# The forward half of the decays' rows made by ScalarE as scaled copies of the mask, in a gated DeltaNet encoder layer

## The chip, the cores and the metric

The kernel runs on one core of a Trainium2 chip. The metric is the device time of one execution in microseconds (us). A core has four compute engines that run side by side, each with its own queue of instructions taken in order: TensorE (PE in the profile: matmuls and transposes; its weight loads, PEld, are shown apart), VectorE (DVE), ScalarE (ACT) and GpSimd (POOL). A fifth, SyncE (SP), only issues DMA transfers here. Engines wait for each other through semaphores.

## The reference, cut to what matters

One layer of a bidirectional encoder is applied to a prompt of 1024 tokens and to a sample of 256, with the same weights. A combined projection feeds two groups of heads: four gated DeltaNet heads, in which a chunked delta rule runs once forward and once backward with separate decays, and four heads of grouped-query attention. An output projection and an MLP follow.

```python
def _gated_delta_chunked(q, k, v, g, beta):          # g <= 0: log of the decay; one direction
    gc = jnp.cumsum(to_chunks(g), axis=-1)
    diff = gc[..., :, None] - gc[..., None, :]
    decay = jnp.where(lower_incl, jnp.exp(jnp.where(lower_incl, diff, 0.0)), 0.0)
    kk = jnp.einsum('bhnid,bhnjd->bhnij', k_beta, kc) * decay
    tri = jnp.eye(CHUNK) + jnp.where(strict, kk, 0.0)
    sol = triangular_solve(tri, [v_beta, k_beta * exp(gc)], lower, unit_diagonal)
    qk = jnp.einsum('bhnid,bhnjd->bhnij', qc, kc) * decay
    ...                                               # scan over chunks with a 128x128 state

def _gated_deltanet(...):
    qkv = silu(depthwise_conv(qkv, conv_w))           # five taps
    q, k = _l2norm(q) * GDN_DK ** -0.5, _l2norm(k)
    o = o_f + flip(o_b)                               # one scan per direction, own g and beta each
    return rmsnorm(o) * gdn_norm_w * silu(z)

def _layer(x, ...):
    p = rmsnorm(x) @ w_in                             # 1024 -> 3088 columns
    mix = concat(_gated_deltanet(...), _axial_gqa(...)) @ w_out
    x = x + rmsnorm(mix)
    return x + rmsnorm(square(relu(rmsnorm(x) @ w_up)) @ w_down)
```

What the change touches is `decay`: for each head, direction and chunk, the exponential of the difference of two running sums of `g`, and zero on the other side of the diagonal.

## The kernel before, in words

**Tiles and stages.** The 1280 tokens lie as ten tiles of 128 (eight of the prompt, two of the sample), and a tile is also the chunk of the delta rule. Values that go through TensorE at full width are split into a rounded high part and the rest (`split`: the high part by ScalarE, L79, the low part by VectorE, L80), and a product takes three matmuls. The kernel runs in stages: the input norm and the gates (until about 85 us), then the projections with everything that prepares the DeltaNet heads (until about 520 us), then attention with the scans, then the output projection and the MLP. The change lies in the second stage.

**The second stage.** It is built from generators that each do one part of the work for one head: K (`gdn_qk`, L453: project, convolve and normalise key and query), V (`gdn_v`, L497: the same for the value), E (`gdn_e`, L511: decays and the matrices A and C made from them), S (`gdn_sub`, L542) and L (`gdn_lev`, L569: the triangular inverse, by VectorE in blocks of 32 first, then by TensorE), and a (`att_proj`, L383: a projection for attention). A table of steps, `ORDER` (L39 to L43), says in which order their pieces are written; `K1 E0 K1 S0`, for instance, writes a piece of head 1's key and query, one of head 0's decays, and so on. A scheduler then orders the instructions of each engine by what they need and by that order, so an edit in one generator can move rows of others in every queue.

**A projection** (`proj_T`, L358 and following): 24 matmuls for each of three stretches of tokens (pt, L370 to L372), copied out by ScalarE (cp, L373). The convolution starts on ScalarE (L443, L444), goes through three steps on VectorE (L446), a sum on GpSimd (L447), a tanh on ScalarE (L448) and a last step on VectorE (L449). TensorE then transposes the result (kt L462, qt L476, vt L505).

**The decays** (`gdn_e`). A head has five groups of two tiles, so there are 20 groups in all. For each group one PSUM tile, pe, of 128 x 512 holds forward (d = 0) and backward (d = 1) for two tiles; two such tiles alternate. Into each half go three matmuls: one writes the mask of large negative values (nmask, L519), two add the differences of the running sums (L525). The latter multiply a constant triangle (strict) with R, which the profile calls ER: the mask of kept positions (`incl`, 128 x 128) times g of the row. `gr` holds g as a high and a low part, so one R has four blocks of 128 x 128: high and low (i) for two tiles (j). Summed along the partitions by the matmul, column c of R becomes the sum of g over the rows between. There is one buffer of R (`bufs=1`), used in turn by the forward and the backward half: the forward half is made by GpSimd, the backward half by VectorE, each in one instruction of 128 x 512 (L521). ScalarE takes the exponential of pe (E, L526). Then for each of the two tiles TensorE makes the products of keys with keys and queries (pk, L531), and VectorE makes A (L532) and C (L534) from pk and E. C goes into the inverse, A to memory in `vis_d`, where the scans fetch it later (vis, L655).

**The start of the third stage.** SP loads the normalised keys, the first queries and the values (ax, L666) and the first chunks of the scans (vis, L655); the former are split (k_hi, q_hi, v_hi) ahead of the first scores (ps_s, L715) and the scans' products (p, L813 and following).

Of the kernel before, what the change touches and what calls it, by code (L numbers as in the profile page):

```python
# [13 lines left out]
AF = mybir.ActivationFunctionType  # L14
ALU = mybir.AluOpType
# [46 lines left out]
def build(ctx, tc, I, O):  # L62
    nc = tc.nc
    V, S, G, T, SP = nc.vector, nc.scalar, nc.gpsimd, nc.tensor, nc.sync
# [9 lines left out]
    def f32(ap):  # L74
        return ap.bitcast(F32)
# [38 lines left out]
    scale = 128.0 ** -0.5  # L114
# [123 lines left out]
    incl = gc.tile([128, 2, 128], F32, name="incl")  # L238
# [92 lines left out]
    gr = gc.tile([128, 2, NT, 8], F32R, name="gr")  # L331
# [5 lines left out]
    for d in range(2):  # L337
        gd = gg[:, :, 4 * d:4 * d + 4]
# [15 lines left out]
    def col(t):  # L354
        return slice(t * 128 + (2 if t >= NPR else 0), t * 128 + (2 if t >= NPR else 0) + 128)
# [155 lines left out]
    def gdn_e(h):  # L511
        qk, sc = qks[h], sca[:, h]

        C = gp.tile([128, NT, 2, 128], F32, tag="C", name="C", bufs=2)
        for t0, n in ((0, 2), (2, 2), (4, 2), (6, 2), (8, 2)):
            E = gp.tile([128, 2, 2, 128], F32, tag="E", name="E", bufs=2)
            pe = tr_tile("pe").rearrange("p (d j c) -> p d j c", d=2, j=2)
            for d in range(2):
                T.matmul(pe[:, d], lhsT=identr, rhs=nmask[:, 1 - d:2 - d].to_broadcast([128, 2, 128]), start=True, stop=False)  # L519
                R = gp.tile([128, 2, 2, 128], F32R, tag="ER", name="ER", bufs=1)  # L520
                (G if d == 0 else V).tensor_tensor(  # L521
                    R, incl[:, d][:, None, None, :].to_broadcast([128, 2, 2, 128]),
                    f32(gr[:, :, t0:t0 + 2, 4 * d + h])[:, :, :, None].to_broadcast([128, 2, 2, 128]), ALU.mult)
                for i in range(2):
                    T.matmul(pe[:, d], lhsT=(r_gt, r_lt)[d], rhs=R[:, i], start=False, stop=(i == 1))  # L525
            S.activation(E, pe, AF.Exp)  # L526
            A = gp.tile([128, 2, 2, 128], F32, tag="A", name="A", bufs=1)
            for j in range(n):
                t = t0 + j
                pk = tr_tile("pk")  # L530
                T.matmul(pk[:, 0:256], lhsT=qk[:, 1, col(t)], rhs=qk[:, :, col(t)], start=True, stop=True)  # L531
                V.tensor_tensor(A[:, j], E[:, :, j], pk[:, None, 0:128].to_broadcast([128, 2, 128]), ALU.mult)  # L532
                for d in range(2):
                    V.scalar_tensor_tensor(C[:, t, d], pk[:, 128:256], sc[:, t, d:d + 1], E[:, d, j], ALU.mult, ALU.mult)  # L534

            SP.dma_start(out=vis_d[h][:, t0:t0 + n, 0], in_=A[:, :, 1])
            SP.dma_start(out=vis_d[h][:, t0:t0 + n, 7], in_=A[:, :, 0])
            if t0 < 8:
                yield
        Cs[h] = C  # L540
# [28 lines left out]
    def gdn_lev(h):  # L569
# [63 lines left out]
        SP.dma_start(out=vis_d[h][:, :, 8], in_=C[:, :, 0])  # L633

    FN = dict(K=gdn_qk, V=gdn_v, E=gdn_e, S=gdn_sub, L=gdn_lev, a=att_proj)
    parts = {}
    for step_ in ORDER.split():
# [752 lines left out]
    for s in range(NS):  # L1390
        n, i = divmod(s, 7)
# [135 lines left out]
```

## Time and profile before

| what | value |
|---|---|
| median of three runs | 1722.2 us (1721.96 to 1723.77) |
| the profiled execution | 1718.87 us |
| its span, first to last instruction | 1717.1 us, mean granted TensorE clock 0.987 |
| TensorE busy (PE) | 1615.6 us, 94% of the span |
| weight loads (PEld) | 1380.5 us, 80% |
| VectorE busy (DVE) | 1276.5 us, 74% |
| ScalarE busy (ACT) | 851.2 us, 50% |
| GpSimd busy (POOL) | 703.1 us, 41% |
| DMA | 252.68 MB, 147 GB/s on average |

The profile is one execution, recorded by the hardware. Shares over the whole span are an average over stages with different limits, so the second stage has to be read by itself. In the rows that follow, `cy<-cp,cw` means that tile cy is written from tiles cp and cw; `x20 | 28.4, 1422` is a count, the busy time of all of them in us and the mean of one in ns; what stands behind it is the idle time of that engine just before them, and the work whose end closed most of it. A row of the timeline has the start in us, the duration in us, the engine and the instruction; in square brackets stands how long the engine had been idle ahead of it and what ended that.

### The profile page before, as it was taken

The numbers are of one execution on the slowest core, as the hardware profiler recorded it, in microseconds if no ns is written. First come the engines' busy times: TensorE is split into PE (matmuls) and PEld (weight loads), VectorE is DVE, ScalarE is ACT, GpSimd is POOL, SyncE is SP. The second block draws the span as 40 slices with busy tenths as digits, with TensorE's granted clock in tenths as the row PEclk, the third lists the DMA queues.
The fourth block names the chain that finished last, engine by engine and source line by source line (L and its number), as shares of the span: only waits on it lengthen the run. The fifth ranks groups of instructions, "written<-read, shape, count | busy, mean of one in ns | idle before, by whom it ended". The sixth has DMA issues, their size and how long they took to land. (4 is left out here: it accounts for less than half of the span.)

```text
span 1717.1 us, 27988 instructions
## 1 busy us (share of the span) xinstructions
PE 1615.6 (94%) x9799; PEld 1380.5 (80%) x9799; DVE 1276.5 (74%) x2570; ACT 851.2 (50%) x1937; POOL 703.1 (41%) x637
## 2 busy tenths in 40 slices
PE   7999899898997999889998999999999999999996
PEld 5777777777776888668877999999998888888885
DVE  7546798996755878885759659555797888887876
ACT  5236567554345767674446446544564333333412
POOL 1212231321114334440103634644335778878852
PEclk9999999999998999999999999999999999999998
DMA  7113335455457766245333545444666444444244
GB/s 221 67 44 108 106 100 143 123 143 154 129 149 241 269 206 193 81 163 168 106 121 116 167 136 177 150 134 138 199 212 209 147 139 148 141 128 147 78 138 150
DMA packets 208779, 252.68 MB, mean 147 GB/s; under 512 B 35073, under 2 KB 163391, under 8 KB 208639
## 3 DMA queue, kind: packets, MB, share of 16 engines
q1 hardware_dynamic: 208495, 250.77, 46.4%
q8 instruction: 77, 1.26, 0.3%
q14 instruction: 63, 0.52, 0.1%
q0 software_dynamic: 144, 0.13, 0.0%
HBM read 159.75 MB, written 91.10 MB: 146 GB/s over the span
## 5 line engine op out<-in xcount | busy, mean ns | idle before, releaser
L1165 PE MATMUL pd<-mh,uhl 128*128 128x320 f32 x892 | 278.0, 312 | 9.8 <-DVE uhl L1156 9.6
L1164 PE MATMUL pd<-mh,uhl 128*128 128x320 f32 x892 | 275.4, 310 | 1.6 <-ACT uhl L1155 1.6
L1166 PE MATMUL pd<-ml,uhl 128*128 128x320 f32 x892 | 276.1, 310 | 0.0
L1313 DVE TENSOR_TENSOR acc<-acc,pd 128x512 f32<-128x512 f32 x330 | 207.3, 679 | 48.6 <-PE pd L1309 48.2
L1307 PE MATMUL pd<-dhi,fhi 128*128 128x512 f32 x490 | 192.2, 392 | 0.7 <-DVE acc L1315 0.7
L1308 PE MATMUL pd<-dl,fhi 128*128 128x512 f32 x490 | 192.3, 392 | 0.0
L1309 PE MATMUL pd<-dhi,flo 128*128 128x512 f32 x490 | 191.9, 392 | 0.0
L1165 PEld LDWEIGHTS pd<-mh,uhl 128*128 128x128 f32 x892 | 168.3, 189 | 12.7 <-DVE uhl L1156 12.7
L371 PE MATMUL pt<-h_lo,whi 128*128 128x512 f32 (+1 forms) x480 | 177.4, 370 | 0.0
L370 PE MATMUL pt<-h_hi,whi 128*128 128x512 f32 (+1 forms) x480 | 177.3, 369 | 0.0
L372 PE MATMUL pt<-h_hi,wlo 128*128 128x512 f32 (+1 forms) x480 | 177.2, 369 | 0.0
L1164 PEld LDWEIGHTS pd<-mh,uhl 128*128 128x128 f32 x892 | 167.8, 188 | 2.7 <-ACT uhl L1155 2.7
L1166 PEld LDWEIGHTS pd<-ml,uhl 128*128 128x128 f32 x892 | 168.3, 189 | 0.0
L1289 ACT CAST fhi<-fr 128x1280 fp32r<-128x1280 f32 x49 | 62.1, 1267 | 200.9 <-PE pd L1308 114.5
L1210 POOL TENSOR_TENSOR s<-u,u 128x320 f32<-128x320 f32 x31 | 29.2, 941 | 254.9 <-ACT u L1174 249.3
L1279 POOL TENSOR_TENSOR dl<-dw,dhi 128x1024 fp32r<-128x1024 f32 x47 | 118.5, 2522 | 28.2 <-ACT dhi L1278 28.2
L1156 DVE TENSOR_TENSOR uhl<-us,uhl 128x512 fp32r<-128x512 f32 x88 | 86.3, 983 | 37.1 <-ACT uhl L1155 36.3
L730 POOL TENSOR_TENSOR P<-P,sm 128x512 f32<-128x512 f32 (+1 forms) x72 | 73.5, 1040 | 95.0 <-DVE sm L728 47.7
L1307 PEld LDWEIGHTS pd<-dhi,fhi 128*128 128x128 f32 x490 | 92.0, 188 | 22.0 <-issue 1.1
L1309 PEld LDWEIGHTS pd<-dhi,flo 128*128 128x128 f32 x490 | 92.0, 188 | 20.7
L1308 PEld LDWEIGHTS pd<-dl,fhi 128*128 128x128 f32 x490 | 92.0, 188 | 20.4
L1173 ACT ACTIVATE u<-u 128x320 f32<-128x320 f32 x128 | 60.2, 470 | 93.0 <-DVE u L1200 39.2
(368 smaller groups left out, 4098.0 us busy)
## 6 DMA issues: line engine op xcount, KB each, us to landing
fr<-r_d SPq DMA_DIRECT2D x49, 640.0 KB, 3.9
vis<-vis_d SPq DMA_DIRECT2D x64, 384.0 KB, 4.1
uraw<-in_w_up SPq DMA_DIRECT2D x22, 1024.0 KB, 5.3
r_d<-s SPq DMA_DIRECT2D x128, 160.0 KB, 1.8
r_d<-u SPq DMA_DIRECT2D x96, 160.0 KB, 1.8
dw<-in_w_down SPq DMA_DIRECT2D x28, 512.0 KB, 4.3
wraw<-in_w_in SPq DMA_DIRECT2D x48, 256.0 KB, 3.9
x<-in_x_prompt SPq DMA_DIRECT2D x16, 512.0 KB, 3.5
```

Of the source, the lines that this page charges most:

```text
L370: T.matmul(pm[:, :n], lhsT=whi, rhs=h_hi[:, k, t0:t0 + n], start=(k == 0), stop=False)
L371: T.matmul(pm[:, :n], lhsT=whi, rhs=h_lo[:, k, t0:t0 + n], start=False, stop=False)
L372: T.matmul(pm[:, :n], lhsT=wlo, rhs=h_hi[:, k, t0:t0 + n], start=False, stop=(k == KD - 1))
L1156: V.tensor_tensor(lo, ua[n][UP[i][0]], f32(hi), ALU.subtract)
L1164: T.matmul(pm, lhsT=w[0][:, k], rhs=mh[b, i][:, k], start=(k == 0), stop=False)
L1165: T.matmul(pm, lhsT=w[1][:, k], rhs=mh[b, i][:, k], start=False, stop=False)
L1166: T.matmul(pm, lhsT=w[0][:, k], rhs=ml[b, i][:, k], start=False, stop=(k == 3))
L1279: last["pool"] = leng.tensor_tensor(lo, raw, f32(hi), ALU.subtract)
L1307: T.matmul(pm, lhsT=r[0][:, k, tk], rhs=w[0][:, k], start=(k == 0), stop=False)
L1308: T.matmul(pm, lhsT=r[0][:, k, tk], rhs=w[1][:, k], start=False, stop=False)
L1309: T.matmul(pm, lhsT=r[1][:, k, tk], rhs=w[0][:, k], start=False, stop=(k == Q - 1))
L1313: last["dve"] = V.tensor_tensor(half(t, d), half(t, d), pm, ALU.add)
```

## The change

For the forward half (d = 0) of each group, the one GpSimd instruction that made R is replaced by four ScalarE instructions, one for each block of 128 x 128: an activation with function Copy that reads the mask `incl` and multiplies each partition's row by a scale of its own, a column of `gr`. The backward half stays one VectorE instruction, and the tile, its single buffer and the matmuls that read it stay as they are.

```diff
@@ -518,9 +518,14 @@
             for d in range(2):
                 T.matmul(pe[:, d], lhsT=identr, rhs=nmask[:, 1 - d:2 - d].to_broadcast([128, 2, 128]), start=True, stop=False)
                 R = gp.tile([128, 2, 2, 128], F32R, tag="ER", name="ER", bufs=1)
-                (G if d == 0 else V).tensor_tensor(
-                    R, incl[:, d][:, None, None, :].to_broadcast([128, 2, 2, 128]),
-                    f32(gr[:, :, t0:t0 + 2, 4 * d + h])[:, :, :, None].to_broadcast([128, 2, 2, 128]), ALU.mult)
+                gd = f32(gr[:, :, t0:t0 + 2, 4 * d + h])
+                if d == 0:
+                    for i in range(2):
+                        for j in range(2):
+                            S.activation(R[:, i, j], incl[:, d], AF.Copy, scale=gd[:, i, j:j + 1])
+                else:
+                    V.tensor_tensor(R, incl[:, d][:, None, None, :].to_broadcast([128, 2, 2, 128]),
+                                    gd[:, :, :, None].to_broadcast([128, 2, 2, 128]), ALU.mult)
                 for i in range(2):
                     T.matmul(pe[:, d], lhsT=(r_gt, r_lt)[d], rhs=R[:, i], start=False, stop=(i == 1))
             S.activation(E, pe, AF.Exp)
```

The instructions of TensorE, VectorE and SP are the same in number (8824, 2573 and 826 in the program); ScalarE goes from 1628 to 1708, GpSimd from 643 to 623. Lines behind the edit are five higher: the matmul of R is L525 before and L530 now, the exponential L526 and L531, pk L531 and L536, C L534 and L539. The scheduler's order differs from the first group of head 0 up to about two thirds of attention and is the same from there on. Three places follow; a number behind x counts rows in a row that are alike.

ScalarE's queue where the second head's groups (E1) begin, before:

```order
L373 COPY cp<-pt 128x256
L526 ACTIVATE E<-pe 128x512
L443 ACTIVATE cy<-cp,cw 128x1282
L444 ACTIVATE qk<-cp,cw 128x1282
L526 ACTIVATE E<-pe 128x512
L373 COPY cp<-pt 128x512
L526 ACTIVATE E<-pe 128x512
L373 COPY cp<-pt 128x512
L79 CAST whi<-wraw 128x512 x2
L373 COPY cp<-pt 128x256
L444 ACTIVATE qk<-cp,cw 128x1282
L548 ACTIVATE Cc<-C 32x640 x4
```

The same place now, with the copies of the mask as rows of L525:

```order
L373 COPY cp<-pt 128x256
L443 ACTIVATE cy<-cp,cw 128x1282
L444 ACTIVATE qk<-cp,cw 128x1282
L79 CAST whi<-wraw 128x512 x2
L531 ACTIVATE E<-pe 128x512
L525 ACTIVATE ER<-incl,gr 128x128 x4
L531 ACTIVATE E<-pe 128x512
L525 ACTIVATE ER<-incl,gr 128x128 x4
L531 ACTIVATE E<-pe 128x512
L525 ACTIVATE ER<-incl,gr 128x128 x4
L448 ACTIVATE qk<-cy 128x1282
L553 ACTIVATE Cc<-C 32x640 x4
```

The start of the convolution has moved ahead of the groups, and three groups stand together, each E ahead of the next group's four copies; behind the last of them comes the tanh.

TensorE's queue at the end of the second head's groups, before (pe and pk belong to the groups, pt to a projection; fifteen more rows of pt follow before the next pe):

```order
L371 MATMUL pt<-h_lo,whi 128x256
L372 MATMUL pt<-h_hi,wlo 128x256
L519 MATMUL pe<-nmask,identr 128x256
L525 MATMUL pe<-ER,strict 128x256 x2
L519 MATMUL pe<-nmask,identr 128x256
L370 MATMUL pt<-h_hi,whi 128x512
L371 MATMUL pt<-h_lo,whi 128x512
L372 MATMUL pt<-h_hi,wlo 128x512
```

The same place now:

```order
L530 MATMUL pe<-ER,strict 128x256 x2
L536 MATMUL pk<-qk 128x256
L519 MATMUL pe<-nmask,identr 128x256
L530 MATMUL pe<-ER,strict 128x256 x2
L519 MATMUL pe<-nmask,identr 128x256
L536 MATMUL pk<-qk 128x256
L530 MATMUL pe<-ER,strict 128x256 x2
L536 MATMUL pk<-qk 128x256
L519 MATMUL pe<-nmask,identr 128x256
L530 MATMUL pe<-ER,strict 128x256 x2
L519 MATMUL pe<-nmask,identr 128x256
L462 MATMUL kt<-ident,qk 128x128 x4
```

Two groups now follow each other with no matmul of a projection between; those matmuls stand elsewhere in the queue.

SP's queue at the change from the second to the third stage, before (L410 stores attention's values, L433 a rotated key, L666 loads a key, query or value, L655 a scan's chunk; the keys take three loads, the fourth is the first queries):

```order
L666 DMA ax<-arot_d 128x512
L410 DMA arot_d<-avn 128x512
L666 DMA ax<-arot_d 128x512
L410 DMA arot_d<-avn 128x512
L410 DMA arot_d<-avn 128x256
L666 DMA ax<-arot_d 128x256
L666 DMA ax<-arot_d 128x512
L433 DMA arot_d<-araw 128x1280
L655 DMA vis<-vis_d 128x512
```

The same place now:

```order
L410 DMA arot_d<-avn 128x512 x2
L410 DMA arot_d<-avn 128x256
L671 DMA ax<-arot_d 128x512 x2
L671 DMA ax<-arot_d 128x256
L660 DMA vis<-vis_d 128x512
L433 DMA arot_d<-araw 128x1280
L660 DMA vis<-vis_d 128x384
L660 DMA vis<-vis_d 128x128
L660 DMA vis<-vis_d 128x512
L660 DMA vis<-vis_d 128x384
L660 DMA vis<-vis_d 128x128
L671 DMA ax<-arot_d 128x512 x3
```

The keys' loads stand together behind the last value stores, and the first queries (the first row of the last x3) come behind six loads of scan chunks.

## The prediction

> **What bounds the kernel now.** I began with busy time in three stretches: the gates and the first head, the middle of the projections, their tail. Columns are busy microseconds, instructions in brackets.
>
> ```profile
> core 0: us, PE busy (x) PEld busy (x) DVE busy (x) ACT busy (x) POOL busy (x), PEclk, DMA share, GB/s
> 85.00:200.00 115.00, 105.51 (x551) 84.40 (x550) 68.18 (x133) 61.96 (x178) 23.02 (x26) 0.99 0.32 89
> 200.00:400.00 200.00, 179.56 (x1418) 144.56 (x1417) 181.65 (x417) 117.74 (x318) 54.63 (x135) 0.97 0.46 126
> ```
>
> From 200 to 400 us TensorE (90% busy) and VectorE (91%) are both nearly full, ScalarE is at 59%, GpSimd at 27%. So here the longest chain changes hands between two engines, and only what makes one of them wait counts. Next the waits of TensorE, and of VectorE for ScalarE, from 85 to 440 us: total, times, longest.
>
> ```profile
> PE pe L519 <- DVE C L534: 7.5, 5, 2.5
> PE vt L505 <- DVE vT L449: 5.7, 3, 2.1
> PE pe L525 <- DVE ER L521: 1.2, 1, 1.2
> ...
> DVE wlo L80 <- ACT whi L79: 11.9, 12, 2.5
> DVE qk L449 <- ACT qk L448: 11.3, 4, 4.5
> ```
>
> TensorE waits for VectorE. For ER it waited once, and that ER was VectorE's: it never waited for GpSimd's rows. VectorE in turn waits for ScalarE's results. Last the groups that the edit touches: count, busy us and mean ns, idle time before them.
>
> ```profile
> L521 POOL TENSOR_TENSOR ER<-incl,gr 128x512 fp32r<-128x512 f32 x20 | 28.4, 1422 | 71.2 <-PE pe L525 69.8 <-DVE wlo L80 1.4
> L467 ACT ACTIVATE kn<-kt,cum 128x128 f32<-128x128 f32 x80 | 22.5, 397 | 0.3 <-DMA vis_d<-kn 0.3
> L443 ACT ACTIVATE cy<-cp,cw 128x1282 f32<-128x1282 f32 x12 | 16.6, 1380 | 2.4 <-DVE qk L449 2.4
> ```
>
> GpSimd's 69.8 us idle before ER is the one ER buffer not yet read, and costs nobody anything unless something needed is queued behind.
>
> **Part by part.** *Added on ScalarE.* Twenty groups get four copies of 128x128 with a scale per row: 80 instructions. The kn row is the same count of the same form, reading PSUM: 22.5 us, 1.12 a group. From below, L443's time per element (16.6/12/1282 = 1.08 ns) gives 80 x 128 x 1.08 = 11 us; from above, 80 full durations of 397 ns give 32 us. I take 22.5, the nearest row. The copies add no wait of their own: the ER buffer comes free with the same matmuls (L525, backward half) that E (L526) waits for, and E stands ahead of the next copies in ScalarE's queue. What they delay is behind them. In the order, 9 of the 20 groups have, as the next row that is not an E, a weight split, a copy of a projection, a tanh or the inverse's first copy, all on somebody's path: 9 x 1.12 = 10.1 us. The other eleven are followed by squares, kn and the like, which the 41% idle time of the stretch hides; without that cover they would cost another 12.3. That idle time absorbs as much of the 10.1, and 59% passes on, since VectorE already waits for ScalarE: **+6.0** (0 to 10.1).
>
> *Removed from GpSimd.* No engine waited for the result, but VectorE was slowed while it was made. Start, us, instruction:
>
> ```profile
> 239.50 1.67 POOL L521 TENSOR_TENSOR ER<-incl,gr 128x512 fp32r<-128x512 f32 x1
> ...
> 127.46 1.68 DVE L446 SCALAR_TENSOR_TENSOR cy<-cp,cw,cy 128x1282 f32<-128x1282 f32 x1 [0.58 <-ACT cy L443]
> ...
> 236.68 0.40 DVE L564 TENSOR_TENSOR Rm<-Rm,prod 80x247 f32<-80x247 f32 x1
> 238.24 1.43 DVE L563 TENSOR_TENSOR prod<-Rm 80x240 f32<-80x240 f32 x1
> 240.19 1.25 DVE L564 TENSOR_TENSOR Rm<-Rm,prod 80x240 f32<-80x240 f32 x1
> ...
> 397.69 1.02 DVE L89 TENSOR_SCALAR nah<-nax 128x10 f32<-128x10 f32 x1
> ```
>
> The two products at 238.24 and 240.19, which take 0.40 otherwise, took 1.43 and 1.25. Twelve VectorE instructions were so lengthened under an ER, from the one at 127.46 to the one at 397.69; each less the median of its shape, they sum to 8.7 us. VectorE is the one waited for about half the time (it and TensorE are equally full), so **-4.3** (-8.7 to 0). The Trainium skill ("SBUF — State Buffer", Who interferes with whom) says that a GpSimd instruction reading SBUF and a VectorE one with two SBUF inputs exclude each other for a whole instruction. By that rule up to all 28.4 us of ER could have stood in VectorE's way, an estimate, half of it -14.2; the trace agrees on who blocks whom and gives 8.7 as the size.
>
> GpSimd's queue also gets shorter. Once a conv sum stood behind an ER:
>
> ```profile
> 176.98 1.60 POOL L521 TENSOR_TENSOR ER<-incl,gr 128x512 fp32r<-128x512 f32 x1 [4.45 <-PE pe L525]
> 178.54 3.40 POOL L447 TENSOR_TENSOR cy<-cy,qk 128x1282 f32<-128x1282 f32 x1
> ```
>
> ScalarE's tanh and then TensorE's transposes wait for that sum. Half of 1.6, as above: **-0.8** (-1.6 to 0).
>
> *Moved: the second head's groups.* Two groups now stand in TensorE's queue with no projection matmul between, at a place where VectorE interleaves the groups with the triangular inverse. VectorE's pace per group there is the distance of its ERs; TensorE's own work per group is the three lower rows over 20.
>
> ```profile
> 212.54 0.68 DVE L521 TENSOR_TENSOR ER<-incl,gr 128x512 fp32r<-128x512 f32 x1
> 226.39 0.68 DVE L521 TENSOR_TENSOR ER<-incl,gr 128x512 fp32r<-128x512 f32 x1
> ...
> L531 PE MATMUL pk<-qk 128*128 128x256 f32 x80 | 26.5, 419 | 3.2 <-DVE prod L563 2.3 <-ACT E L526 0.7
> L525 PE MATMUL pe<-ER,strict 128*128 128x256 f32 x80 | 18.2, 307 | 1.2 <-DVE ER L521 1.2
> L519 PE MATMUL pe<-nmask,identr 128*128 128x256 f32 x40 | 13.0, 326 | 7.8 <-DVE C L534 7.5
> ```
>
> Pace 13.85/2 = 6.9, work 57.7/20 = 2.9: 4.05 us of idle in each group, 8.1 for two. The projection matmuls that stood there run later instead, where TensorE had these gaps:
>
> ```profile
> 242.90 0.66 PE L462 MATMUL kt<-ident,qk 128*128 128x128 f32 x4 [1.87 <-DVE qk L449]
> 258.16 1.10 PE L531 MATMUL pk<-qk 128*128 128x256 f32 x4 [2.30 <-DVE prod L563]
> 274.53 0.66 PE L505 MATMUL vt<-ident,vT 128*128 128x128 f32 x4 [2.03 <-DVE vT L449]
> ```
>
> They fill up to 6.2 us: **+1.9** (-6.2, if VectorE keeps ahead, to +8.1). A gap also slows what follows it:
>
> ```profile
> 201.39 0.39 PE L371 MATMUL pt<-h_lo,whi 128*128 128x512 f32 x1
> 204.30 0.38 PE L519 MATMUL pe<-nmask,identr 128*128 128x256 f32 x1 [2.52 <-DVE C L534]
> 206.71 0.63 PE L371 MATMUL pt<-h_lo,whi 128*128 128x512 f32 x1
> ```
>
> After 2.52 us of idle the same matmul takes 0.63 for 0.39. New gaps and filled ones both carry this, so I let it cancel. The Trainium skill ("TensorE: Matmul & The Clock Gate", HAM oscillation) puts the limit at gaps over about 3.4 us. By that only the new gaps would pay; the row at 204.30 shows a shorter gap paying, and decides.
>
> *Moved: the change to attention.* SP's queue now has the first query load behind the last value stores and six vis loads.
>
> ```profile
> 526.08 0.80 PE L715 MATMUL ps_s<-k_hi,q_hi 128*128 128x512 f32 x1 [6.22 <-ACT q_hi L79]
> 530.59 1.06 PE L813 MATMUL p<-vis 128*128 128x128 f32 x4
> ...
> 524.20 2.78 SPq L655 DMA_DIRECT2D vis<-vis_d  x6
> ```
>
> TensorE waits 6.22 us for that query today; six issues take 2.78, so the wait grows by as much, less four L813 matmuls put ahead in the meantime (1.06 us): **+1.7** (0 to +2.8).
>
> The sum is 6.0 - 4.3 - 0.8 + 1.9 + 1.7 = +4.5. The profiled execution took 1718.87 (span 1717.1 and 1.77 around it): 1723.4. The median of the runs lies 3.3 higher, at 1722.2: **1726.7**. Nothing after the attention's first two thirds is reordered, and TensorE is full there, so I let the difference stand to the end.
>
> **Rivals.** *A, the relief wins (faster).* ScalarE's idle time takes the copies, at most 1.0 of the 10.1 passes, and VectorE gains the whole 8.7: -8.7 - 0.8 + 1.0 + 1.9 + 1.7 = -4.9, so 1717.3. For it: VectorE is the fullest engine from 200 to 400. Against: the 23 us that VectorE waits for ScalarE between 85 and 440 us. It decides once under 2.4 of the 10.1 passes and the relief is whole. This is also what the port rule of the Trainium skill's "SBUF — State Buffer" leads to. *B, nothing measurable.* Groups wait for whichever of the two full engines is behind, the terms cancel: 1722.2, 0.2% (3.4 us) either way, about what a measurement of this kernel can tell from no change. For it: no wait for GpSimd's ER exists, and TensorE can lose little to an engine 59% busy. *C, ScalarE's queue becomes the wait.* All 10.1 pass, nothing of the 8.1 comes back: 10.1 - 4.3 - 0.8 + 8.1 + 1.7 = +14.8, so 1737. For it: three groups of copies stand in a row ahead of a tanh. Against: ScalarE's 82 idle us in the stretch. That the edit does not do what it says would mean copies much dearer than kn; that is C as well, at up to 32 us.
>
> **How the numbers follow.** My forecast (slower by 3.4 to 9 us) has 0.36, A 0.28, B 0.27, C 0.09. So faster 0.28, same 0.27, slower 0.45. The range takes A with no loss at the two moved places (-4.9 - 3.6 = -8.5, 1713.7, less a little) up to C: 1712 to 1737. The forecast's own range is 1725.6 to 1731.
>
> **What would show it.** Right: about 80 ER copies of 22 us in all on ScalarE; ScalarE above 63% between 200 and 400; VectorE's lengthened products gone; gaps of 3 to 5 us on TensorE inside the second head's groups; a first ps_s wait above 6.2. Wrong: VectorE's wait for whi and tanh unchanged with fewer TensorE gaps than now (A), or all gaps merely moved (B).

## The result: slower by 1.8%

The changed kernel takes 1753.2 us (median of 3 runs, 1752.9 to 1754.7) against 1722.2: a ratio of 1.0177, 95% interval 1.0159 to 1.0195, or 31 us. That lies outside the predicted range (1712 to 1737), on the side that had 0.45. A ratio compares a kernel with runs of the kernel before made beside it, so it need not be that of the medians given.

The profiled execution has a span of 1751.1 us. The stretches of the prediction, and the two behind them, in the changed kernel (columns as there):

```profile
85.00:200.00 115.00, 107.06 (x562) 86.72 (x560) 71.34 (x139) 70.85 (x208) 15.57 (x23) 0.99 0.31 84
200.00:400.00 200.00, 168.78 (x1407) 134.04 (x1410) 167.76 (x396) 125.81 (x342) 30.75 (x117) 0.89 0.44 118
400.00:520.00 120.00, 109.12 (x957) 86.59 (x958) 72.68 (x195) 43.88 (x141) 15.24 (x36) 0.94 0.42 122
520.00:560.00 40.00, 28.16 (x160) 22.60 (x158) 13.10 (x27) 14.43 (x45) 6.96 (x3) 0.82 0.61 195
```

From 200 to 400 us TensorE falls from 90% to 84% busy and VectorE from 91% to 84%: both wait more, so neither became the bound. ScalarE, which got the work, reaches 62.9%, where above 63% was forecast. The granted clock in that stretch is 0.89 for 0.97. The waits of the same window, 85 to 440 us, and the new group:

```profile
DVE wlo L80 <- ACT whi L79: 29.4, 9, 7.7
DVE qk L449 <- ACT qk L448: 13.9, 5, 4.5
PE pe L519 <- DVE C L539: 7.1, 4, 3.2
PE qt L476 <- ACT gj L379: 6.1, 1, 6.1
PE pk L536 <- DVE qk L449: 3.4, 1, 3.4
```

```profile
L525 ACT ACTIVATE ER<-incl,gr 128x128 fp32r<-128x128 f32 x80 | 26.7, 406 | 0.0
```

The copies cost 26.7 us of ScalarE where 22.5 were forecast. TensorE waits for R twice, 0.4 us in all, whichever engine makes it. VectorE's waits for weight splits and tanh have grown (29.4 for 11.9 and 13.9 for 11.3 us), and TensorE has two new single waits, of 6.1 and 3.4 us.

TensorE runs the same 9799 rows in both traces. Its busy time goes from 1615.6 to 1629.7 us and the rest of the span from 101.5 to 121.4, so of the 34 us by which the profiled execution is longer, 20 are idle time and 14 are the same matmuls taking longer, at a mean granted clock of 0.973 for 0.987.

To see where the time goes I took TensorE's matmuls in both traces, counted each with the spacing its kind has in a run without gaps, and noted when the same amount of work had been done (a reckoning of work). Changed kernel less before, in us:

| time before | work done | changed less before | what lies between |
|---|---|---|---|
| 177 | 150 | -1.6 | |
| 216 | 180 | -4.9 | the changed kernel is ahead |
| 236 | 200 | +8.9 | end of the second head's groups |
| 323 | 270 | +9.4 | |
| 334 | 280 | +21.1 | fourth head's query, third head's value |
| 460 | 380 | +12.9 | 8 us won back |
| 471 | 390 | +20.3 | attention's projections, prk |
| 515 | 430 | +23.1 | |
| 591 | 490 | +33.6 | change to attention |
| 726 | 610 | +33.5 | nothing more |

So there are four places. Two are those of the prediction, at 14 and 10 us instead of 1.9 and 1.7; two it didn't have. The sizes of these two, 11.7 and 7.4 us here, hang on the spacing that is taken for each kind: with the median of all spacings in the trace they come out at 16.0 and 10.6, and more is won back between them. What the first three share is seen in the busy time of the projections alone (tile pt) in three stretches, before and then changed:

```profile
core 0: us, PE busy (x), PEclk, DMA share, GB/s
...
220.00:235.00 15.00, 13.41 (x62) 1.00 0.14 40
...
325.00:345.00 20.00, 14.05 (x66) 0.91 0.43 111
...
460.00:485.00 25.00, 23.03 (x110) 1.00 0.46 139
```

```profile
core 0: us, PE busy (x), PEclk, DMA share, GB/s
...
220.00:235.00 15.00, 0.42 (x1) 0.66 0.15 44
...
325.00:345.00 20.00, 2.37 (x21) 0.64 0.37 103
...
460.00:485.00 25.00, 12.30 (x60) 0.80 0.30 104
```

Before, projections that wait for nobody fill TensorE's queue beside the groups and the convolutions. Now they stand elsewhere, and where VectorE's, GpSimd's and ScalarE's chains are long, TensorE has nothing else in its queue. Counting the projection matmuls that ran ahead of the same row in both traces says where they went. From the second head's third group to the third head's first mask 81 ran before and 34 run now; of the 47 that are missing, 17 had been done ahead (ahead of that third group 440 have run for 423, which fits the lead of 4.9 us) and 30 come later. At the second place, from the first of the fourth head's query transposes to the first of the third head's value transposes, 69 ran before and 7 run now, and all of the missing come later. At the third, behind attention's last prk rows, 28 ran before and none now, and all had been done ahead. At the first place the gaps are these rows of the changed kernel; before, TensorE is idle for 0.1 us over the same work:

```profile
230.08 0.58 PE L519 MATMUL pe<-nmask,identr 128*128 128x256 f32 x1 [3.17 <-DVE C L539]
...
233.65 1.11 PE L462 MATMUL kt<-ident,qk 128*128 128x128 f32 x4 [2.35 <-DVE qk L449]
```

### The profile page after: what moved, and what is told of

The parts are those of the page before. It is cut to its first block, busy times and chain, and to the rows that moved or that the text cites. A ratio compares the mean times of both kernels' runs of the same rounds, so it can differ in the third digit from the quotient of the medians.

```text
span 1751.1 us, 28001 instructions
## 1 busy us (share of the span) xinstructions
PE 1629.7 (93%) x9799; PEld 1390.0 (79%) x9799; DVE 1275.6 (73%) x2570; ACT 873.8 (50%) x2017; POOL 671.3 (38%) x617
## 5 line engine op out<-in xcount | busy, mean ns | idle before, releaser
L1170 PE MATMUL pd<-mh,uhl 128*128 128x320 f32 x892 | 278.2, 312 | 10.3 <-DVE uhl L1161 10.1
```

The lines of the kernel that those rows point to most:

```text
L1170: T.matmul(pm, lhsT=w[1][:, k], rhs=mh[b, i][:, k], start=False, stop=False)
```

## Experiments

**How an order is held.** The order of all five queues was recorded from each of the two programs, and an edge that only sets the order of issue (no semaphore, no wait) was put from each instruction to its predecessor in the record. The forward half's instructions have no edge and stand where the scheduler puts them. Apart from these, the rows of every engine in run 1's trace stand in the order of the kernel before, and those of run 2 in the order of the changed kernel. At the end of the program (excerpt):

```diff
+    for line in zlib.decompress(base64.b85decode(HELD)).decode().splitlines():
+        e, *runs = line.split()
+        q = [i for i in nc.cur_bb.bb.instructions if str(i.engine) == "EngineType." + e ... and i.name not in FREE]
...
+                    tc.add_manual_dep(q[k], prev.name, mybir.DependencyInfo(
+                        mybir.DependencyClass.NoSync, mybir.DependencyReason.DATA), reason="held order")
```

Theory O: the time is lost by the new order of the queues, whichever engine makes the rows. Rival E: it is lost by ScalarE's copies.

**1. The edit in the old order.**

> The edit as it is (four ScalarE copies for the forward half), but every engine's queue held to the order it had before; only the copies are free to stand where the scheduler puts them. Theory O (the loss of 31 us is the new order of the queues): 1715 to 1727 us, within 0.3% of before, with no TensorE wait over 3 us between 215 and 240 or between 320 and 350 us. Rival E (the loss is ScalarE's added 25 us of copies, wherever they stand): 1745 us or more.

Measured: 1721.3 us, 1.0002 of before (0.9991 to 1.0012). TensorE's longest wait is 0.7 us between 215 and 240 and 2.1 between 320 and 350, and the projections are where they were (tile pt, this kernel):

```profile
220.00:235.00 15.00, 13.53 (x53) 1.00 0.26 71
325.00:345.00 20.00, 14.92 (x72) 1.00 0.56 155
460.00:485.00 25.00, 22.57 (x108) 1.00 0.45 133
```

**2. The old engine in the new order.** The edit is undone (excerpt):

```diff
-                            S.activation(R[:, i, j], incl[:, d], AF.Copy, scale=gd[:, i, j:j + 1])
+                (G if d == 0 else V).tensor_tensor(R, ...)
```

> The other corner: GpSimd makes the forward half as before, and every engine's queue is held to the order that the changed kernel has; only GpSimd's 20 instructions are free. Theory O: 1745 to 1760 us, with the changed kernel's long TensorE waits near 225, 335, 472 and 545 us. Rival E: 1718 to 1727 us.

Measured: 1754.7 us, 1.0203 (1.0179 to 1.0228). Together the two settle it: with the old order held, moving the work to ScalarE costs nothing that can be measured; with the engine held, the order costs 35 us with GpSimd's rows and some 30 with ScalarE's copies (1.0177 against 1.0002). The intervals of these last two overlap. Rival E falls. No run held the old order and changed nothing else, but run 10 is near to it, at 0.9998.

**3. and 4. Price and relief, each alone, in the old order.** ScalarE does the copies as well, into a tile D that nobody reads (3); the forward half is made once, and all groups read that tile, so that 19 groups lack their own decays (4):

```diff
+                    D = gp.tile([128, 2, 2, 128], F32R, tag="ED", name="ED", bufs=1)
+                            S.activation(D[:, i, j], incl[:, d], AF.Copy, scale=gd[:, i, j:j + 1])
```

```diff
+                if d == 0:
+                    R = R0
```

> The price of the copies alone: GpSimd and VectorE make R as before, and ScalarE makes the four copies a second time into a tile that nobody reads, at the places that they have in the run of the edit in the old order; all queues are held to the old order. Theory O: 0 to 6 us over before, 1722 to 1728. Rival E: 20 us or more over before.

> The relief alone: the forward half is made once, by GpSimd, and all 20 groups read that one tile (the decays of the forward direction are left out of the computation but for one group's); queues held to the old order. Theory O: 0.8 to 9 us under before, 1713 to 1721, by VectorE's products that GpSimd no longer lengthens. If the relief is worth nothing: 1720 to 1724. Rival E says nothing of this one.

Measured: the copies alone 1724.8 us, 1.0023 (1.0012 to 1.0035), +3.9 us; without the forward half 1714.1 us, 0.9952 (0.9935 to 0.9969), -8.3 us. Both are as expected. They don't add up to run 1: 3.9 - 8.3 = -4.4 against +0.3. Run 4 also frees the one R buffer of its forward use, so that VectorE's ER no longer waits at all (9.1 us before); whether that is the 4.7 us between them was not separated.

**5. to 7. Old order up to a cut, then the new one**, with ScalarE's copies: a queue is the old record's part ahead of the cut, followed by what is left of the new record.

> ScalarE's copies; all queues in the old order up to the 190th group of three projection matmuls (about 250 us, behind the second head's groups), then what is left in the new order. Theory P (the loss sits at separate places, each with its own wait: near 225, 335, 472 and 545 us): the first place is gone, which leaves what the trace lost after it, 33 - 7 = 26 us: about 1747 us. Rival W (one early loss, and the later waits only follow from it): 1727 us or less.

> The same with the cut at the 310th group of projection matmuls, about 360 us, behind the third head's groups and the fourth head's query. Theory P: 33 - 20 = 13 us are left, about 1734 us. Rival W: 1724 us or less.

> The same with the cut at the 460th group of projection matmuls, about 505 us: only the change to attention is in the new order. Theory P: 33 - 23 = 10 us over before, about 1731 us. The prediction's own term for this place was 1.7 (0 to 2.8): 1721 to 1724. Rival W: 1722.

Measured: 1757.6 (ratio 1.0225), 1760.7 (1.0236) and 1728.3 us (1.0056, 1.0035 to 1.0077). The first two miss both theories. The same reckoning of work shows why: the cut itself costs, 9 us behind 250 us and about 25 us behind 360 us, where TensorE waits 6.8 and 7.05 us in one piece. That the new order takes work for done that the old one had left for later would explain it, and was not tested. Behind the join the places come back, each with its size: from work 270 to 280 the first of the two loses 12.1 us (changed kernel 11.7), from work 380 to 390 they lose 7.5 and 7.4 (changed kernel 7.4). So the places don't hang on what went before them, which is against rival W; theory P's totals missed because a join has a price of its own. The third is as theory P has it: the change to attention costs 9.6 us by the ratio. By the reckoning it is 1.9 us behind before at work 430 and 9.5 at 610, so its join costs next to nothing.

**8. New up to 212 us, then old.**

> The other way round: the new order up to its 150th group of projection matmuls, about 212 us, where the changed kernel was 4.9 us ahead of before, then the old order. Theory P: the lead is kept, about 1716 us. Rival L (the lead is work done early that the old order then waits for): 1720 to 1724 us.

Measured: 1714.1 us, 0.9965 (0.9952 to 0.9979): 6 us faster than before by the ratio, some 36 faster than the changed kernel by the two ratios. The projections are back in their places (tile pt, this kernel):

```profile
220.00:235.00 15.00, 14.04 (x68) 1.00 0.18 52
...
325.00:345.00 20.00, 13.70 (x66) 0.91 0.42 103
...
460.00:485.00 25.00, 21.56 (x100) 1.00 0.50 142
```

**9. The same with GpSimd's rows**, the edit undone as in run 2.

> The faster mixture of orders (new up to about 212 us, then old) with GpSimd making the forward half as in the kernel before. If the 5 us won there are the order's alone: 1713 to 1716 us, as with ScalarE's copies. If they are the engine's (rival A of the prediction, VectorE no longer lengthened by GpSimd): 1719 us or more.

Measured: 1719.6 us, 0.9988 (0.9976 to 0.9999). That is the time named for the engine (1719 or more), though the order is still worth some 2 us without it; by the ratios of runs 8 and 9, whose intervals just overlap, the engine is 4 of the 6 us. The spans of the two profiled executions, 1711.2 and 1712.6, say 1.4, but this kernel's profiled execution (1714.35 us) is the second shortest of twelve. So ScalarE's copies may be a small gain in this order, up to some 4 us and not clear of noise, and they are nothing in the old one.

**10. The clock behind a long wait**, on the kernel before in its own order:

```diff
+            for _ in range(34 if not pend[0] and not halves else 0):
+                T.matmul(pm[:, 0:128], lhsT=ident, rhs=ident, start=True, stop=True)
```

> The price of the lowered clock behind one long wait, on the kernel before: 34 transposing matmuls of the identity (128x128), whose result the first scores overwrite, stand in TensorE's queue in the 6.2 us in which it waits for the first queries; all else in the old order. If the lowered clock costs time there (granted 0.50 to 0.76 between 525 and 535 us): the clock stays at 1.00 and 2 to 4 us are won, 1715 to 1717. If VectorE and ScalarE set the pace there anyway: 0, 1719 us, with the clock up all the same.

Measured: 1720.1 us, 0.9998 (0.9986 to 1.0010). The windows of before, then of this kernel:

```profile
525.00:530.00 5.00, 3.79 (x8) 2.59 (x9) 1.42 (x3) 0.62 (x1) 1.28 (x1) 0.50 0.97 326
530.00:535.00 5.00, 4.55 (x21) 3.73 (x21) 3.43 (x9) 3.60 (x10) 1.22 (x2) 0.76 0.79 268
```

```profile
525.00:530.00 5.00, 5.00 (x42) 4.75 (x41) 0.76 (x2) 1.02 (x2) 1.27 (x1) 1.00 0.95 287
530.00:535.00 5.00, 4.55 (x23) 3.11 (x21) 3.70 (x9) 3.39 (x9) 0.76 (x1) 1.00 1.02 356
```

The clock stays at 1.00 and nothing is won beyond the 2 us that the interval leaves open. The added matmuls ran 7.8 us, about 1 us past the queries' arrival, so at most that much was hidden. Behind them, from 535 to 540 us, VectorE is busy for 4.83 of 5 us before and for all 5 here, which fits the second expectation. At this place the lowered clock is a sign of the wait and not its price; at the others it wasn't tried, and the 14 us by which the changed kernel's matmuls take longer are the most that it can have cost TensorE there.

**11. One instruction moved in the new order.** The timeline of the changed kernel at the place of the fourth head's query and the third head's value, which is the third of the four vT (the expectation below calls it the fourth head's) (excerpt):

```profile
327.46 0.28 PE L519 MATMUL pe<-nmask,identr 128*128 128x256 f32 x1
...
331.14 1.19 PE L536 MATMUL pk<-qk 128*128 128x256 f32 x2 [3.41 <-DVE qk L449]
...
337.06 0.28 ACT L379 ACTIVATE gj<-qt 128x128 bf16<-128x128 f32 x1
...
337.86 2.88 POOL L447 TENSOR_TENSOR cy<-cy,vT 128x1282 f32<-128x1282 f32 x1 [2.89 <-DVE prod L568]
...
338.07 2.75 DVE L569 TENSOR_TENSOR Rm<-Rm,prod 80x60 f32<-80x60 f32 x1
...
340.77 1.27 ACT L448 ACTIVATE vT<-cy 128x1282 f32<-128x1282 f32 x1 [3.34 <-POOL Rm L570]
341.87 0.22 DVE L569 TENSOR_TENSOR Rm<-Rm,prod 80x60 f32<-80x60 f32 x1
341.95 0.26 ACT L379 ACTIVATE gj<-qt 128x128 bf16<-128x128 f32 x1
342.35 1.12 PE L476 MATMUL qt<-ident,qk 128*128 128x128 f32 x4 [6.12 <-ACT gj L379]
```

TensorE's next four transposes need the buffer that the fourth square (gj, 341.95) reads. That square stands behind the value's tanh, which waits for GpSimd's sum; the sum in turn holds up VectorE's product (2.75 us for one that takes 0.22 else). The tanh was put behind three of the squares and a weight split in ScalarE's recorded queue. In the kernel only the record (HELD) differs; as a line of Python on that queue:

```diff
+a.remove(tanh); a.insert(a.index(whi) + 1, tanh)
```

> The changed kernel in its own order with one instruction moved: the tanh of the fourth head's value, which stands in ScalarE's queue ahead of the last squares of qt and waits 3.3 us for GpSimd's sum, goes behind three of those squares and a weight split. Theory H (an instruction that waits at the head of an in-order queue keeps TensorE from its next transposes): the 6.1 us wait near 336 us shrinks by about 4, 1747 to 1751 us. Rival V (VectorE's long chain sets the pace there whatever ScalarE does first): 1752 to 1755.

Measured: 1749.6 us, 1.0167 (1.0148 to 1.0187), 3.6 us under the changed kernel by the medians and 1.7 by the ratios; the intervals of the two overlap, so the place itself has to say it. This kernel there:

```profile
333.97 1.12 PE L476 MATMUL qt<-ident,qk 128*128 128x128 f32 x4 [0.45 <-ACT kn L467]
336.75 1.12 PE L476 MATMUL qt<-ident,qk 128*128 128x128 f32 x4 [1.66 <-ACT gj L379]
```

The wait of 6.12 is 1.66. By the reckoning of work it is 1.1 us ahead of the changed kernel ahead of this place and 3.7 behind it, so 2.6 of the 4.5 us won on the spot last; the profiled execution is 4.8 shorter. So theory H holds for this wait; that the whole time falls is not shown, and the other waits of the place, 3.4 us for qk above all, stay.

**12. SP's queue alone** in the new order from 505 us on: SP's record is that of run 7, the other four are those of run 1.

```diff
+p = dict(old, SP=old_then_new_505["SP"])
```

> ScalarE's copies, old order everywhere but for SP's queue, which from the change to attention on (about 505 us) stands in the new order: keys behind the value stores, the first queries behind six loads of scan chunks. The compute engines keep the first scores ahead of the scans. Theory S (SP's order alone makes the 9 us that the mixture with all queues new lost there): 1728 to 1731 us. Rival T (the prediction's term: six issues later, 1.7 us at most 2.8, and the rest is TensorE's and ScalarE's queues, in which the scans' first steps stand ahead of the first scores): 1722 to 1725 us.

Measured: 1733.2 us, 1.0070 (1.0052 to 1.0087). SP's queue and TensorE's first scores in this kernel:

```profile
519.05 2.55 SPq L410 DMA_DIRECT2D arot_d<-avn  x3
521.70 2.62 SPq L671 DMA_DIRECT2D ax<-arot_d  x3
...
525.75 3.64 SPq L660 DMA_DIRECT2D vis<-vis_d  x5
529.49 1.32 SPq L671 DMA_DIRECT2D ax<-arot_d  x3
```

```profile
534.33 0.79 PE L720 MATMUL ps_s<-k_hi,q_hi 128*128 128x512 f32 x1 [13.48 <-ACT q_hi L79]
```

In the kernel before the loads of SP are these, three of keys and, last, that of the first queries:

```profile
517.00 0.34 SPq L666 DMA_DIRECT2D ax<-arot_d  x1
518.44 0.43 SPq L666 DMA_DIRECT2D ax<-arot_d  x1
520.66 2.04 SPq L666 DMA_DIRECT2D ax<-arot_d  x2
```

SP's order alone makes a loss of 12 us: theory S, some 2 us above its range. The first keys leave 4.7 us later (one of them this kernel was late already), since all three loads now stand behind the last value store, which waits for the last transposes; the queries leave some 8 us later, behind keys and six loads of scan chunks. TensorE waits 13.5 us for 6.2, which is 7.3 of the 12. With the compute engines' new order as well the wait is another one. In the changed kernel the scans' first steps stand ahead of the first scores in TensorE's queue, and they wait, for the split keys and for a scan's chunk; the first scores then wait for nothing:

```profile
550.30 0.77 PE L818 MATMUL p<-vis 128*128 128x128 f32 x2 [6.15 <-DVE k_lo L80]
553.20 0.80 PE L818 MATMUL p<-vis 128*128 128x128 f32 x2 [2.13 <-DMA vis<-vis_d]
...
558.85 0.80 PE L720 MATMUL ps_s<-k_hi,q_hi 128*128 128x512 f32 x1
```

Run 7, where the queues stand so too, loses 9.6 us, and its interval overlaps with that of this run. The opposite mixture, SP old and the others new, was not tried.

**13. An earlier join.**

> The new order up to its 128th group of projection matmuls, about 195 us, where the lead was already 4.4 to 4.9 us, then the old order: a check that the lead is won before 195 us and can be kept whole. If the place of the join doesn't matter: 1713 to 1716 us, as with the join at 212. If the lead is given back by the join (2.2 us of it were at 212): 1711 to 1713 with less of it lost, or up to 1720 with more.

Measured: 1718.7 us, 0.9982 (0.9970 to 0.9994): still faster than before, by half as much as with the join at 212, so more of the lead was lost than at that join. In the changed kernel's trace 4.5 us of the lead are there at 191 us; how much of it lasts depends on the join.

## Why the prediction was wrong

**Engines: right, in the old order.** The copies were put at +6.0 (0 to 10.1) and cost 3.9 in the old order; the relief of VectorE and of GpSimd's queue at -5.1 (-10.3 to 0) and was 8.3 where the rows are not made at all. Their sum, +0.9, was measured as +0.3. That ScalarE's idle time takes most of the copies is what run 3 shows. In the changed kernel itself the relief is hardly there: VectorE's four groups L446, ER, products and sums (57.4, 15.5, 43.3 and 51.6 us before, 167.8 in all) take 162.4 in run 1, but 166.4 in the changed kernel, where GpSimd's conv sums lengthen the inverse's products and sums beside them by 9.9 us in all (each less the shortest of its shape), for 5.6 in run 1; the 2.75 us row is one of them. The Trainium skill ("SBUF — State Buffer", Who interferes with whom) has the rule for it, the exclusive lock of the two engines' shared ports; the row agrees. It is the new order that lets them fall together more often, not the missing rows: in run 2, where GpSimd makes its rows, it is 10.5 us.

**"Moved: the second head's groups", +1.9 (-6.2 to +8.1): the step that failed.** It took two groups, gave each its own idle time (8.1 us), let the displaced projections win 6.2 of it back in later gaps, and put the slowed matmuls behind a gap at nothing ("so I let it cancel"). Measured are about 14 us between 216 and 236. The idle time was sized well: TensorE is idle for 9.2 us where it was idle for 0.1. The rest, some 5 us, is TensorE's work taking longer, at a granted clock of 0.50 from 225 to 238 us: new gaps and filled ones did not cancel. And nearly nothing was won back: of the 47 displaced matmuls 17 had been done ahead, and with the other 30 behind this place at most some 1.5 us came back until the next one. For 15 us no filler was left (13.41 us of projections before, 0.42 now), while the groups run at VectorE's pace, with the convolution's steps in between. This is read from the traces: run 8 brings the old order of all five queues back, and the loss goes with it, but no run put TensorE's queue or its projections back alone.

**"Moved: the change to attention", +1.7 (0 to 2.8): the right queue, the wrong size, and not the wait that was named.** SP's queue alone is enough for the loss (run 12), but only the six issues were counted; the three key loads behind the value stores and their landing were not. In the changed kernel TensorE waits there for the keys and for a scan's chunk and not, as forecast, longer for the first queries. 9.6 us in run 7.

**What was not looked for.** The order differs from 109 to 619 us of the kernel before, and two places of it were priced. Two others cost 11.7 and 7.4 us (16.0 and 10.6 by the other spacing). "Nothing after the attention's first two thirds is reordered, and I let the difference stand" was right for what comes after, and no ground for what lies between.

**The rivals.** A (faster, by VectorE's gain) has nearly its time in run 8, -0.35%, and by the ratios of run 9 the engine may be 4 of the 6 us there, in another order than the edit gives; that VectorE's gain is what does it was not separated. B is run 1. C (ScalarE's queue becomes the wait) has the sign and not the cause: 10.1 of its 14.8 us were copies, and the copies alone cost 3.9 (run 3). A rival "the reordering as such, summed over all of its places" was missing.

## What to carry to other kernels

Where a scheduler orders the queues, an edit of a few instructions is two changes, and the order can be the larger: here 30 to 35 us against nothing measurable in the old order. Before pricing the instructions, count in both orders what filler each stretch has beside its longest chain (here the projections between two waits), over all of the reordered program, not at the places that catch the eye. To judge the edit itself, hold the old order with issue-only edges and run it; then a faster order can be looked for by itself.

## What the hardware showed

The clock was lowered without any long gap. In the changed kernel, second head's groups, windows of TensorE alone:

```profile
219.00:221.00 2.00, 1.12 (x6) 1.00 0.00 0
221.00:223.00 2.00, 0.74 (x4) 1.00 0.00 0
223.00:224.00 1.00, 0.35 (x2) 1.00 0.67 197
224.00:225.00 1.00, 0.82 (x4) 0.94 0.22 66
225.00:226.00 1.00, 0.32 (x1) 0.50 0.00 0
```

Until it fell at 225 us no gap had been longer than 1.18 us, but TensorE had been busy for only 3.0 of the 6 us since 219. The Trainium skill ("TensorE: Matmul & The Clock Gate", HAM oscillation) speaks of gaps over about 3.4 us; here many short ones did the same. And run 10 shows that a clock held up needn't be worth anything: behind that wait it stayed at 1.00, and the time was the same within 2 us.
